# A decoder layer on one core: the expert layer's VectorE work in another order, with sums taken a slot later and v operands made in two steps

## The chip, the cores and the metric

The kernel runs on one core of one Trainium2 chip. The metric is the device time of one execution in microseconds. A core has five engines that each run their own instruction queue in order: TensorE (PE, matrix products into PSUM; its weight loads have a row of their own, PEld), VectorE (DVE), ScalarE (ACT), GpSimd (POOL) and SyncE (SP, which here only issues transfers). Sixteen DMA engines move data between HBM and the on-chip memory. An engine that meets an instruction whose input isn't there yet stands still, and everything behind it in its queue waits too.

## What is computed

One layer over 512 tokens of width 2048: norm, projections, a gated recurrent mixer, a sparse attention mixer, an output projection, and then an expert layer (PEER). Each token picks 128 of 16384 experts (8 heads of 16), each expert being one row of `u` and one row of `v`. The change touches only this layer:

```python
def peer(x, wq, keys1, keys2, u, v):
    ...
    expert = jnp.take_along_axis(cand_i, pos, axis=-1).reshape(t, -1)      # (512, 128)
    gate = jax.nn.softmax(top_s, axis=-1).reshape(t, -1)
    def chunk(args):
        xc, ec, gc = args
        z = jnp.einsum('cd,ced->ce', xc, u[ec])
        act = jax.nn.gelu(z, approximate=False) * gc
        return jnp.einsum('ce,ced->cd', act, v[ec])
    ...
```

## The kernel before

The expert layer is computed in two ways at once. For the first 176 tokens (three row sets of 128, 32 and 16 tokens) the chosen rows are fetched: one indirect transfer brings 128 rows of 2048 numbers, 1.05 MB, into one of three buffers named `rows` (`issue`), and one DVE operation of `use` multiplies and sums it. There are 352 such gathers. `gather(rate)` adds `rate` to a credit at each slot and runs one `use` for every whole credit, so the gathers are spread evenly between the other work.

For the other 336 tokens every expert is computed: `u_tile(i)` is z = gelu(u x) for the 128 experts of tile i, in two pieces of 24 matmuls, and `v_piece(g, pc)` multiplies the gated z of the eight tiles of group g with one piece of v, 24 matmuls again. A matmul here has a 128x128 weight and 336 columns. There are 128 u tiles and 16 v groups of 16 pieces. In this document a slot is the time of one piece. The order is u0 to u33, v0, then two u tiles between two v groups up to v3, u40 to u42, v4, and from there eight u tiles and one v group in turn, v14 behind u122 and v15 at the end.

Full precision comes from splitting each factor into a rounded hi part and the lo part that is left, and three products (`mm3`; lines L167, L168 and L169 are its hi times hi, hi times lo and lo times hi). A weight piece is loaded by SP into `raw`, ACT makes `whi` (L107), DVE subtracts to get `wlo` (L108), and PE uses both. `Pieces.next` gives PE its piece and, ahead of that piece's matmuls in program order, makes both parts of the piece two further on and loads three beyond that. For tiles u0 to u4 POOL makes the lo part in DVE's place.

z isn't ready for v when it leaves PE: it must be multiplied by the gates, and split. `make_a(i)` does all of it at once: DVE multiplies (L962), ACT makes `ah` (L107), DVE makes `al` (L108). `make_some` calls it in the u slots, one tile a slot in the steady part and three a slot in the tiles up to u39. z of the first 40 tiles is spilled to HBM and read back by `load_z`. The gates in expert order are the G matrix; while tiles u5 to u26 run, PE builds it from one-hot vectors that DVE makes for four tokens at a time (`g_batch`; `e1` L1020, `e2` L1021), and it is stored to HBM and read back in a block per group by `load_g`.

A v piece's 128x336 sum is added to `yT` by DVE straight behind its matmuls (L990), but for every fourth piece, which stays in PSUM. When the gathers have ended, after tile u124, `side_load` adds the partial sums of the two small row sets together in five halving steps, and `side_out` norms and stores one row set behind each of u125 to u127. `quarter` transposes, adds and norms the dense tokens at the end.

Of the kernel before, what the change touches and what calls it, by code (L numbers as in the profile page):

```python
# [17 lines left out]
D = 2048  # L18
# [20 lines left out]
class Pieces:  # L39


    def __init__(self, nc, raws, parts, plan, split, load_ahead, split_ahead):
        self.nc, self.raws, self.parts, self.plan, self.split = nc, raws, parts, plan, split
        self.la, self.sa = load_ahead, split_ahead
        self.raw, self.out = {}, {}
        self.loaded = self.done = self.cur = 0
        self.after = {}
        self.extra = None

# [12 lines left out]
    def split_to(self, n):  # L62
        while self.done < min(n, len(self.plan)):
            self.load_to(self.done + 1)
            r, w = self.raw.pop(self.done)
            hi = self.parts.tile([128, 1024], F32R, name="whi")
            lo = self.parts.tile([128, 1024], F32R, name="wlo")
            self.split(hi[:, :w], lo[:, :w], r[:, :w], self.plan[self.done][2])
            self.out[self.done] = (hi, lo)
            self.done += 1  # L70

    def next(self, key, ahead=None):
        assert self.plan[self.cur][0] == key, (self.plan[self.cur][0], key)
        i = self.cur
        self.cur += 1
        self.load_to(i + 1)
        self.split_to(i + 1 + (self.sa if ahead is None else ahead))
        self.load_to(i + 1 + self.la)
        return self.out.pop(i)


def program(tc, a, out):
# [68 lines left out]
    W = Pieces(nc, raws, parts, plan, split, 5, 2)  # L151
# [780 lines left out]
    def u_tile(i, fill, mid=None):  # L932
        p = pw.tile([128, 512], F32, name="pw")
        for hf in range(2):
            whi, wlo = W.next(("u", i, hf))
            for j in range(8):
                k = hf * 8 + j
                cs = slice(j * 128, (j + 1) * 128)
                mm3(p[:, :ND], whi[:, cs], wlo[:, cs], *dense(k), k == 0, k == KT - 1)
                if mid and j % 2:  # L940
                    mid()
            step(fill)
        z = ep["z"].tile([128, ND], F32, name="z")
        nc.scalar.activation(z, p[:, :ND], AF.Gelu)
        if i < NZ:
            nc.scalar.dma_start(zd[i], z)
        else:
            ZR[i] = z
# [5 lines left out]
    def load_z(i):  # L954
        if i < NZ:
            z = ZR[i] = ep["z"].tile([128, ND], F32, name="z")
            nc.sync.dma_start(z, zd[i])

    def make_a(i):
        z = ZR.pop(i)  # L960
        zv = z.rearrange("p (c t) -> p c t", c=NCH)
        nc.vector.tensor_tensor(out=zv, in0=zv, in1=GI[i // 8][:, :, i % 8], op=OP.mult)  # L962
        ah = ep["zp"].tile([128, ND], F32R, name="ah", bufs=9)
        al = ep["zp"].tile([128, ND], F32R, name="al", bufs=9)
        split(ah, al, z)
        AR[i] = (ah, al)


    RES = {}

    def v_piece(g, pc):
# [12 lines left out]
        if res and g == NG - 1:  # L984
            yo = RES[pc] = ep["z"].tile([128, ND], F32, name="z")
# [3 lines left out]
        elif not res:  # L989
            nc.vector.tensor_tensor(out=yo, in0=yo, in1=p[:, :ND], op=OP.add)  # L990
# [13 lines left out]
    def g_batch(tok):  # L1004
# [43 lines left out]
    ep = {"z": pool(zs, "zearly", 2, side="right")}  # L1048

# [95 lines left out]
    RG = 0.3  # L1145
# [4 lines left out]
    def gather_v():  # L1150
        gather(rate)
# [27 lines left out]
    ep["z"] = pool(ev, "z", 8, side="right")  # L1179
# [11 lines left out]
    side = deque((w, st[4], st[5], st[6]) for w, st in enumerate(SETS))  # L1191

    def side_load():
        nc.gpsimd.dma_start(gl, bcast_row(a["gfin"], D))

        for _, y, R, _ in list(side)[1:]:
            n = 64
            while n >= R:
                x = lp.tile([128, D], F32, name="rows", bufs=3)
                nc.gpsimd.dma_start(x[:n], y[n:2 * n])  # L1200
                nc.vector.tensor_tensor(out=y[:n], in0=y[:n], in1=x[:n], op=OP.add)
                n //= 2
# [4 lines left out]

    def side_out():
        w = side.popleft()
        for d in range(4):  # L1210
            normed(*w[:3], d)
        final_out(*w)

    def normed(w, X, P, d):
# [3 lines left out]
        sq = ep["z"].tile([128, ND], F32, name="z")[:, :256].bitcast(BF16)  # L1218
# [34 lines left out]
    def make_some(n, stop):  # L1253
        while n and made[0] < stop and made[0] in ZR:
            make_a(made[0])
            made[0] += 1
            n -= 1
# [3 lines left out]
    rate = (len(seq) - st_["used"]) / (2 * (124 - i) + KT * (NG - 1))  # L1261
    for kind, n in order[i:]:
        if kind == "u":
            if n == U0 - 3:
                load_g(0)
            if n == U0 - 2:
# [11 lines left out]
            if n > 124 and side:  # L1278
                side_out()
        else:  # L1280
            make_some(8, n * 8 + 8)
            assert made[0] >= n * 8 + 8
# [3 lines left out]
            for pc in range(KT):  # L1286
                if pc == 2:
                    load_g(n + 1)
                if pc == 9:
# [6 lines left out]
    assert not side  # L1296

    g = NG - 1
    for pc in range(KT):
        v_piece(g, pc)  # L1300
# [66 lines left out]
```

## Time and profile before

| | us |
|---|---|
| median of 3 runs | 3595.46 |
| lowest and highest | 3591.84, 3596.07 |
| the profiled execution | 3595.78 |
| its span | 3594.0 |

The profile follows one execution. The span runs from its first to its last recorded instruction; the execution's own time is 1.78 us longer. Rows count only busy time of an engine, so what an engine lost shows as the difference between a stretch and its busy time, and the view of the waits puts each idle piece down to the instruction that ended it. The stretches by the trace's clock: one-hot stage about 1500 to 1717, the early groups (v0 to v3) 1770 to 2210, the steady groups 2210 to 3446, the end 3446 to 3577, and then the last transposes, norms and stores.

### The profile page before, as it was taken

To read this page: it belongs to the slowest core of one execution; us is meant where nothing else is said; L and a number is where in the kernel's file an instruction comes from. 1 tells how busy PE (TensorE), PEld (TensorE's weight loads), DVE (VectorE), ACT (ScalarE), POOL (GpSimd) and SP (SyncE) were. 2 spreads that over 40 slices of the span, in tenths; PEclk is the share of its full clock that TensorE was granted. 3 is DMA by queue.
4 is the path that set the end of the run, shared out by engine and by line. 5 is a ranking of instruction groups with operands and counts; after the bars stand their busy time and mean duration, and the time that the engine had idled before them with its cause. 6 is when DMAs were issued, how large, how long until landed. Compare 5 with 4: busy or idle time off the path is not lost.

```text
span 3594.0 us, 50928 instructions
## 1 busy us (share of the span) xinstructions
PE 3451.9 (96%) x19965; PEld 3200.5 (89%) x19965; DVE 2664.0 (74%) x4378; ACT 1296.8 (36%) x1873; POOL 790.7 (22%) x595
## 2 busy tenths in 40 slices
PE   8999999999999999999999999999999999999977
PEld 7988888888888888899999889999999999999977
DVE  6778755444443369999778888888888888878875
ACT  5555554333332332344333322333333333323333
POOL 4200000000010055500122232332332232223210
PEclk9999999999999999999999999999999999999989
DMA  5323322222224352577899998999999999999973
GB/s 191 117 88 100 96 93 90 84 79 77 82 95 141 116 150 89 169 259 264 340 348 352 359 377 332 379 356 355 377 368 348 348 387 357 344 351 382 358 265 112
DMA packets 215137, 860.35 MB, mean 239 GB/s; under 512 B 22992, under 2 KB 65104, under 8 KB 166640
## 3 DMA queue, kind: packets, MB, share of 16 engines
q1 hardware_dynamic: 147824, 439.21, 34.2%
q0 software_dynamic: 59440, 388.97, 27.9%
q10 hardware_dynamic: 7632, 28.91, 2.1%
q8 instruction: 156, 2.56, 0.3%
q14 instruction: 85, 0.70, 0.1%
HBM read 811.54 MB, written 36.64 MB: 236 GB/s over the span
## 4 chain that ended last, share of the span: by engine, by line
PE 42%; DVE 11%; issue 5%; ACT 3%; DMA 3%; POOL 1%; SPq 0%; ACTq 0%; POOLq 0%; DVEq 0%
PE pw L169 10%; PE pw L167 10%; PE pw L168 10%; DVE wlo L108 4%; ACT whi L107 2%; DVE rows L1130 2%; PE pg L1029 2%; DVE x1A L1136 2%; PE pr L167 2%; PE pr L168 2%; PE pr L169 2%; PE acc L169 2%; PE acc L168 2%; PE acc L167 2%; DVE z L962 1%
## 5 line engine op out<-in xcount | busy, mean ns | idle before, releaser
L108 DVE TENSOR_TENSOR wlo<-raw,whi 128x1024 fp32r<-128x1024 f32 (+1 forms) x712 | 864.0, 1217 | 470.3 <-ACT whi L107 468.0
L107 ACT CAST whi<-raw 128x1024 fp32r<-128x1024 f32 (+1 forms) x752 | 780.1, 1040 | 984.9 <-PE pw L168 364.1
L169 PE MATMUL pw<-h2m,wlo 128*128 128x336 f32 x2048 | 658.2, 321 | 46.6 <-DVE wlo L108 40.8
L167 PE MATMUL pw<-h2m,whi 128*128 128x336 f32 x2048 | 662.9, 324 | 19.0 <-ACT whi L107 18.4
L167 PE MATMUL pw<-ah,whi 128*128 128x336 f32 x1536 | 492.8, 321 | 24.3 <-ACT whi L107 12.8
L169 PE MATMUL pw<-ah,wlo 128*128 128x336 f32 x1536 | 493.1, 321 | 11.6 <-DVE wlo L108 11.6
L168 PE MATMUL pw<-al,whi 128*128 128x336 f32 x1536 | 491.2, 320 | 0.5
L167 PE MATMUL acc<-hTh,whi 128*128 128x512 f32 (+1 forms) x1152 | 444.9, 386 | 0.8 <-ACT nts L370 0.8
L168 PE MATMUL acc<-hTl,whi 128*128 128x512 f32 (+1 forms) x1152 | 443.2, 385 | 2.3 <-DVE hTl L270 2.3
L169 PE MATMUL acc<-hTh,wlo 128*128 128x512 f32 (+1 forms) x1152 | 444.0, 385 | 0.0
L169 PEld LDWEIGHTS pw<-h2m,wlo 128*128 128x128 f32 x2048 | 389.1, 190 | 59.1 <-DVE wlo L108 52.5
L167 PEld LDWEIGHTS pw<-h2m,whi 128*128 128x128 f32 x2048 | 390.4, 191 | 26.3 <-ACT whi L107 26.0
L168 PE MATMUL pw<-h2m,whi 128*128 128x336 f32 x1024 | 326.8, 319 | 0.0
L1116 POOL DMA_INDIRECT rows<-in_u,ex x128 | 191.3, 1495 | 613.0 <-DVE rows L1130 550.9
L168 PE MATMUL pw<-h2r,whi 128*128 128x336 f32 x1024 | 325.8, 318 | 0.0
L167 PEld LDWEIGHTS pw<-ah,whi 128*128 128x128 f32 x1536 | 294.1, 191 | 28.6 <-ACT whi L107 14.5
L1136 DVE SCALAR_TENSOR_TENSOR x1A<-rows,zgA,x1A 128x2048 f32<-128x2048 f32 x128 | 300.2, 2345 | 10.1 <-DMA rows<-in_v,ex 10.1
L169 PEld LDWEIGHTS pw<-ah,wlo 128*128 128x128 f32 x1536 | 293.6, 191 | 15.3 <-DVE wlo L108 14.9
L1130 DVE SCALAR_TENSOR_TENSOR rows<-rows,h2g 128x2048 f32<-128x2048 f32 x128 | 292.3, 2284 | 10.2 <-DMA rows<-in_u,ex 10.1
L168 PEld LDWEIGHTS pw<-al,whi 128*128 128x128 f32 x1536 | 294.2, 192 | 2.6 <-DVE al L108 2.6
L1116 POOL DMA_INDIRECT rows<-in_v,ex x128 | 184.7, 1443 | 436.0 <-DVE x1A L1136 345.6
L168 PEld LDWEIGHTS acc<-hTl,whi 128*128 128x128 f32 x1152 | 216.4, 188 | 45.4 <-DVE hTl L270 3.0
(363 smaller groups left out, 6027.6 us busy)
## 6 DMA issues: line engine op xcount, KB each, us to landing
raw<-in_ut SPq DMA_DIRECT2D x256, 512.0 KB, 6.3
raw<-in_vt SPq DMA_DIRECT2D x256, 512.0 KB, 8.0
raw<-in_wt SPq DMA_DIRECT2D x144, 512.0 KB, 3.5
gd<-stg ACTq DMA_DIRECT2D x12, 1792.0 KB, 7.0
gi<-gd SPq DMA_DIRECT2D x16, 1344.0 KB, 17.1
raw<-in_wo SPq DMA_DIRECT2D x32, 512.0 KB, 3.2
raw<-in_wq SPq DMA_DIRECT2D x32, 512.0 KB, 3.2
raw<-in_wukv SPq DMA_DIRECT2D x16, 512.0 KB, 3.2
```

What stands on the lines that cost most here:

```text
L107: nc.scalar.copy(hi, src)
L108: (lo_eng or nc.vector).tensor_tensor(out=lo, in0=src, in1=hi.bitcast(F32), op=OP.subtract)
L167: nc.tensor.matmul(p, ahi, bhi, start=start, stop=False)
L168: nc.tensor.matmul(p, ahi, blo, start=False, stop=False)
L169: nc.tensor.matmul(p, alo, bhi, start=False, stop=stop)
L962: nc.vector.tensor_tensor(out=zv, in0=zv, in1=GI[i // 8][:, :, i % 8], op=OP.mult)
L1029: nc.tensor.matmul(p[:, j * 128:(j + 1) * 128], e1[:, j], e2[:, j], start=True, stop=True)
L1116: nc.gpsimd.indirect_dma_start(out=r, out_offset=None, in_=a[kind], in_offset=bass.IndirectOffsetOnAxis(ap=SETS[w][0][:, s:s + 1], axis=0))
L1130: nc.vector.scalar_tensor_tensor(r, r, 1.0, hg, op0=OP.mult, op1=OP.mult, accum_out=zg[:, s:s + 1])
L1136: nc.vector.scalar_tensor_tensor(y, r, zg[:, s:s + 1], y, op0=OP.mult, op1=OP.add)
```

## The change

- `Pieces` makes hi and lo parts apart. From u0 on (`defer`) `next` asks ACT for the hi part of the piece two ahead, and `finish`, at the end of a slot, makes its lo part and loads five pieces further in place of three where the two extra buffers exist.
- `make_a` is cut in three: `make_mul` in one slot, `make_hi` and `make_lo` in the next.
- `v_piece` hands its addition back, and the next slot does it first.
- `slot` sets DVE's order in a slot: the last piece's sums, multiplies, gathers, `al`, and then the lo part.
- Gather rates: 0.55 a slot in place of 0.3 in the one-hot stage, none in tiles u32 to u39, 0.756 in other u slots and 0.826 in v slots; what is left after u121 is done there at once (before: after u124).
- `e1` of four tokens is made by one operation.
- The halving sums, norms and stores of the row sets are a generator, `folds`, one step in each slot from u122 on; the two sets' steps alternate.
- `load_g(0)` and the first `load_z` stand a tile earlier, later ones two pieces earlier; z has a name of its own for tiles that are spilled.

```diff
@@ class Pieces @@
...
+    def finish(self):
+        n = self.cur + self.sa
+        self.lo_to(n)
+        self.load_to(n + 3 + (NRAW2 if self.extra else 0))
@@ def next @@
-        self.split_to(i + 1 + (self.sa if ahead is None else ahead))
-        self.load_to(i + 1 + self.la)
+        if self.defer:
+            self.lo_to(i + 1)
+            self.hi_to(i + 1 + self.sa)
+        else:
+            self.split_to(i + 1 + (self.sa if ahead is None else ahead))
+            self.load_to(i + 1 + self.la)
         return self.out.pop(i)
@@ def v_piece @@
         elif not res:
-            nc.vector.tensor_tensor(out=yo, in0=yo, in1=p[:, :ND], op=OP.add)
+            return [lambda: nc.vector.tensor_tensor(out=yo, in0=yo, in1=p[:, :ND], op=OP.add)]
+        return []
@@ def one_hot @@
+            if js[0] == 0:
+                B = [128, 4, 128]
+                nc.vector.tensor_tensor(out=e1, in0=iota[:, None, :].to_broadcast(B),
+                                        in1=iT[:, 0, j0:j0 + 4, None].to_broadcast(B), op=OP.is_equal)
             for j in js:
                 t = j0 + j
-                nc.vector.tensor_scalar(e1[:, j], iota, iT[:, 0, t:t + 1], None, op0=OP.is_equal)
...
+    W.finish()
+    W.defer = True
...
-    RG = 0.3
+    RG = 0.55
...
+    def folds():
         nc.gpsimd.dma_start(gl, bcast_row(a["gfin"], D))
+        n, got = 64, []
+        while True:
+            for y, x, m in got:
+                nc.vector.tensor_tensor(out=y[:m], in0=y[:m], in1=x[:m], op=OP.add)
...
+            n //= 2
+            yield
...
+    def slot(rate, muls=()):
+        while adds:
+            adds.popleft()()
+        old = list(fin)
+        fin.clear()
+        for i in muls:
+            make_mul(i)
+        for i in old:
+            make_hi(i)
+        gather(rate)
+        for i in old:
+            make_lo(i)
...
-    rate = (len(seq) - st_["used"]) / (2 * (124 - i) + KT * (NG - 1))
+    between = range(U0 - 2, NZ)
+    nu = 2 * len([n for n in range(i, 122) if n not in between])
+    RU = (len(seq) - st_["used"] - 0.07 * KT * (NG - 1)) / (nu + KT * (NG - 1))
+    RV = RU + 0.07
...
             def fill():
-                gather_v()
-                make_some(3 if n < NZ else 1, min((group + 1) * 8, n))
+                stop = min((group + 1) * 8, n)
+                k = 3 if n in between else 1
+                muls = [j for j in range(made[0], min(made[0] + k, stop)) if j in ZR]
+                made[0] += len(muls)
+                slot(0 if n in between else RU, muls)
+                if n > 121:
+                    next(side, None)
             u_tile(n, fill)
-            if n == 124:
+            if n == 121:
                 while st_["used"] < len(seq):
                     use()
-                side_load()
...
-                v_piece(n, pc)
-                step(gather_v)
+                add = v_piece(n, pc)
+                slot(RV)
+                adds.extend(add)
+                W.finish()
```

Three places show the moved order on DVE. The first is a u group in the steady part, behind v13; before, each slot begins with the lo part and then has a gather, a multiply and `al` of the same z:

```order
L108 TENSOR_TENSOR wlo_29406<-raw_29308,whi_29405 128x1024
L1136 SCALAR_TENSOR_TENSOR yB_12283<-rows_29336,zgS0_12285,yB_12283 128x2048
L962 TENSOR_TENSOR z_28721<-z_28721,gi_28925 128x336
L108 TENSOR_TENSOR al_29440<-z_28721,ah_29439 128x336
L108 TENSOR_TENSOR wlo_29444<-raw_29343,whi_29443 128x1024
L1136 SCALAR_TENSOR_TENSOR yB_12283<-rows_29371,zgS0_12285,yB_12283 128x2048
L962 TENSOR_TENSOR z_28787<-z_28787,gi_28925 128x336
L108 TENSOR_TENSOR al_29478<-z_28787,ah_29477 128x336
```

The same place after the change:

```order
L79 TENSOR_TENSOR wlo_29135<-raw_28994,whi_29134 128x1024
L992 TENSOR_TENSOR z_28479<-z_28479,gi_28685 128x336
L1180 SCALAR_TENSOR_TENSOR yB_12283<-rows_29093,zgS0_12285,yB_12283 128x2048
L79 TENSOR_TENSOR wlo_29167<-raw_29028,whi_29166 128x1024
L992 TENSOR_TENSOR z_28548<-z_28548,gi_28685 128x336
L1180 SCALAR_TENSOR_TENSOR yB_12283<-rows_29128,zgS0_12285,yB_12283 128x2048
L1003 TENSOR_TENSOR al_29229<-z_28479,ah_29228 128x336
L79 TENSOR_TENSOR wlo_29201<-raw_29062,whi_29200 128x1024
```

The multiply now opens the slot, `al` (of z_28479) comes a slot behind its multiply, and the lo part closes the slot.

The second place is DVE at the first multiplies, those for v0; before, they stand in u32:

```order
L108 TENSOR_TENSOR wlo_15509<-raw_15390,whi_15508 128x1024
L1130 SCALAR_TENSOR_TENSOR rows_15452,zgA_12284<-rows_15452,h2g_8662 128x2048
L962 TENSOR_TENSOR z_15491<-z_15491,gi_15419 128x336
L108 TENSOR_TENSOR al_15543<-z_15491,ah_15542 128x336
L962 TENSOR_TENSOR z_15493<-z_15493,gi_15419 128x336
L108 TENSOR_TENSOR al_15548<-z_15493,ah_15547 128x336
L962 TENSOR_TENSOR z_15495<-z_15495,gi_15419 128x336
L108 TENSOR_TENSOR al_15553<-z_15495,ah_15552 128x336
L108 TENSOR_TENSOR wlo_15557<-raw_15426,whi_15556 128x1024
```

After the change they begin in u31, whose two slots have one multiply each:

```order
L992 TENSOR_TENSOR z_15206<-z_15206,gi_15137 128x336
L1174 SCALAR_TENSOR_TENSOR rows_15128,zgA_12284<-rows_15128,h2g_8662 128x2048
L79 TENSOR_TENSOR wlo_15224<-raw_15062,whi_15223 128x1024
L992 TENSOR_TENSOR z_15208<-z_15208,gi_15137 128x336
L1174 SCALAR_TENSOR_TENSOR rows_15197,zgA_12284<-rows_15197,h2g_8662 128x2048
L1003 TENSOR_TENSOR al_15286<-z_15206,ah_15285 128x336
L79 TENSOR_TENSOR wlo_15258<-raw_15099,whi_15257 128x1024
L992 TENSOR_TENSOR z_15210<-z_15210,gi_15137 128x336
L992 TENSOR_TENSOR z_15212<-z_15212,gi_15137 128x336
```

Lo parts and one gather a slot still lie between them in u31; from u32 on the gathers are gone and three multiplies stand together. The z loads are issued right ahead of the tile of the first multiply in both.

The third place is the end of the gathers on DVE; before, no gather is left over and five halving sums stand together between two lo parts, near u125:

```order
L108 TENSOR_TENSOR al<-z,ah 128x336
L1201 TENSOR_TENSOR yB<-yB,rows 64x2048
L1201 TENSOR_TENSOR yB<-yB,rows 32x2048
L1201 TENSOR_TENSOR h2gB<-h2gB,rows 64x2048
L1201 TENSOR_TENSOR h2gB<-h2gB,rows 32x2048
L1201 TENSOR_TENSOR h2gB<-h2gB,rows 16x2048
L108 TENSOR_TENSOR wlo<-raw,whi 128x1024
```

After the change, behind u121 (x13 is thirteen of them in a row):

```order
L79 TENSOR_TENSOR wlo<-raw,whi 128x1024
L1180 SCALAR_TENSOR_TENSOR h2gB<-rows,zgS_12286,h2gB 128x2048 x13
L79 TENSOR_TENSOR wlo<-raw,whi 128x1024
L1239 TENSOR_TENSOR yB<-yB,rows 64x2048
L1239 TENSOR_TENSOR h2gB<-h2gB,rows 64x2048
L79 TENSOR_TENSOR wlo<-raw,whi 128x1024 x2
```

The halving sums come two to a slot, and thirteen gathers stand between two lo parts.

## Rows read from the trace of the kernel before

**Rows 1.** Busy time, share of the span and instructions of each engine.
```profile
PE 3451.9 (96%) x19965; PEld 3200.5 (89%) x19965; DVE 2664.0 (74%) x4378; ACT 1296.8 (36%) x1873; POOL 790.7 (22%) x595
```
**Rows 2.** Windows: stretch, us, busy PE, PEld, DVE, ACT, POOL, PEclk, DMA, GB/s.
```profile
1450.00:1500.00 50.00, 43.27 (x246) 42.36 (x245) 44.94 (x161) 17.17 (x22) 30.77 (x24) 0.86 0.33 112
...
1500.00:1717.00 217.00, 216.18 (x1573) 215.64 (x1573) 210.73 (x680) 94.72 (x139) 28.12 (x29) 1.00 0.72 262
...
1770.00:2210.00 440.00, 405.71 (x2495) 395.89 (x2494) 362.22 (x362) 135.19 (x172) 123.11 (x85) 0.95 0.93 358
...
2210.00:3446.00 1236.00, 1200.84 (x7680) 1183.47 (x7679) 1066.51 (x964) 388.57 (x487) 375.76 (x270) 0.99 0.94 362
...
3446.00:3577.00 131.00, 105.13 (x663) 103.23 (x663) 81.33 (x108) 47.47 (x85) 6.98 (x11) 0.91 0.45 143
...
2395.00:2454.00 59.00, 59.00 (x386) 59.00 (x385) 53.18 (x47) 17.21 (x17) 21.00 (x13) 1.00 1.01 399
2454.00:2518.00 64.00, 61.09 (x390) 59.61 (x389) 53.26 (x56) 21.72 (x32) 14.61 (x14) 1.00 0.89 335
```
**Rows 3.** PE's waits (us, times, longest): first 1770-2210, then 2210-3446, then 3446-3577.
```profile
PE pw L167 <- ACT whi L107: 21.2, 7, 7.1
...
PE pw L169 <- DVE wlo L108: 26.8, 35, 5.8
...
PE pw L169 <- DVE wlo L108: 19.4, 3, 18.4
```
**Rows 4.** Timeline 2213-2218: start, us, instruction, [idle before <-releaser].
```profile
2214.87 0.50 DVE L962 TENSOR_TENSOR z<-z,gi 128x336 f32<-128x336 f32 x1
...
2215.40 0.47 ACT L107 CAST ah<-z 128x336 fp32r<-128x336 f32 x1 [4.53 <-DVE z L962]
...
2215.78 1.04 ACT L107 CAST whi<-raw 128x1024 fp32r<-128x1024 f32 x1
...
2215.91 0.51 DVE L108 TENSOR_TENSOR al<-z,ah 128x336 fp32r<-128x336 f32 x1 [0.54 <-ACT ah L107]
...
2216.86 1.23 DVE L108 TENSOR_TENSOR wlo<-raw,whi 128x1024 fp32r<-128x1024 f32 x1 [0.44 <-ACT whi L107]
```
**Rows 5.** DVE's waits in 1770-3446 (us, times, longest).
```profile
DVE wlo L108 <- ACT whi L107: 94.3, 140, 3.4
...
DVE al L108 <- ACT ah L107: 67.7, 120, 0.9
...
DVE yT L990 <- PE pw L169: 38.3, 40, 3.5
...
DVE z L962 <- DMA z<-zd: 7.7, 1, 7.7
```
**Rows 6.** DVE's groups in 2210-3446: busy, mean ns | idle before, releaser.
```profile
L108 DVE TENSOR_TENSOR wlo<-raw,whi 128x1024 fp32r<-128x1024 f32 x320 | 389.8, 1221 | 68.6 <-ACT whi L107 67.6 <-PE pw L168 0.4
...
L1136 DVE SCALAR_TENSOR_TENSOR x1A<-rows,zgA,x1A 128x2048 f32<-128x2048 f32 x94 | 220.5, 2346 | 7.1 <-DMA rows<-in_v,ex 7.1
...
L990 DVE TENSOR_TENSOR yT<-yT,pw 128x336 f32<-128x336 f32 x120 | 59.8, 498 | 26.5 <-PE pw L169 26.1
```
**Rows 7.** DVE's timeline in the one-hot stage.
```profile
1604.39 0.28 DVE L1020 TENSOR_SCALAR e<-iota,gT 128x128 f32<-128x128 f32 x1
1604.59 0.34 DVE L1021 TENSOR_SCALAR e<-iota,gT 128x128 f32<-128x128 f32 x1
```
**Rows 8.** A 128x512 operation of DVE, near the end (L1244), as a group.
```profile
L1244 DVE TENSOR_TENSOR rows<-rows,pw 128x512 f32<-128x512 f32 x8 | 5.4, 684 | 3.8 <-PE pw L1243 3.8
```
**Rows 9.** DMA in 1770-3446: totals, then gathers (count, median us from issue to landing).
```profile
DMA packets 141296, 604.63 MB, mean 361 GB/s; under 512 B 13328, under 2 KB 44110, under 8 KB 98473
...
rows<-in_v,exS POOLq DMA_INDIRECT x48, 9.6
```
**Rows 10.** DVE's timeline 3000-3016: two gathers in a row.
```profile
3006.93 2.34 DVE L1136 SCALAR_TENSOR_TENSOR x1A<-rows,zgA,x1A 128x2048 f32<-128x2048 f32 x1
...
3010.32 2.35 DVE L1136 SCALAR_TENSOR_TENSOR x1A<-rows,zgA,x1A 128x2048 f32<-128x2048 f32 x1
```

More of the change, by code (lines that the diff above doesn't have):

```diff
@@ L955, in load_z, with make_mul, make_hi, make_lo @@
         if i < NZ:
-            z = ZR[i] = ep["z"].tile([128, ND], F32, name="z")
+            z = ZR[i] = ep["z"].tile([128, ND], F32, name="z", bufs=8)
             nc.sync.dma_start(z, zd[i])
-    def make_a(i):
-        z = ZR.pop(i)
+    mul, fin = deque(), deque()
+    def make_mul(i):
+        z = ZR[i]
         zv = z.rearrange("p (c t) -> p c t", c=NCH)
         nc.vector.tensor_tensor(out=zv, in0=zv, in1=GI[i // 8][:, :, i % 8], op=OP.mult)
-        ah = ep["zp"].tile([128, ND], F32R, name="ah", bufs=9)
-        al = ep["zp"].tile([128, ND], F32R, name="al", bufs=9)
-        split(ah, al, z)
+        fin.append(i)
+    def make_hi(i):
+        ah = ep["zp"].tile([128, ND], F32R, name="ah", bufs=8)
+        al = ep["zp"].tile([128, ND], F32R, name="al", bufs=8)
         AR[i] = (ah, al)
+        nc.scalar.copy(ah, ZR[i])
+    def make_lo(i):
+        ah, al = AR[i]
+        nc.vector.tensor_tensor(out=al, in0=ZR.pop(i), in1=ah.bitcast(F32), op=OP.subtract)
     RES = {}
+    adds = deque()
     def v_piece(g, pc):
@@ L984, in v_piece @@
         if res and g == NG - 1:
-            yo = RES[pc] = ep["z"].tile([128, ND], F32, name="z")
+            yo = RES[pc] = ep["z"].tile([128, ND], F32, name="z", bufs=8)
             nc.scalar.copy(yo, p[:, :ND])
@@ L1190, in program @@
     XD = []
-    side = deque((w, st[4], st[5], st[6]) for w, st in enumerate(SETS))
-    def side_load():
+    def folds():
         nc.gpsimd.dma_start(gl, bcast_row(a["gfin"], D))
[L1196 to L1202, printed above, removed]
+        n, got = 64, []
+        while True:
+            for y, x, m in got:
+                nc.vector.tensor_tensor(out=y[:m], in0=y[:m], in1=x[:m], op=OP.add)
+            got = []
+            for st in SETS[1:]:
+                if n >= st[5]:
+                    x = lp.tile([128, D], F32, name="rows", bufs=3)
+                    nc.gpsimd.dma_start(x[:n], st[4][n:2 * n])
+                    got.append((st[4], x, n))
+            if not got:
+                break
+            n //= 2
+            yield
         for row, P in CHK:
@@ L1206, in side_load @@
             XD.append(x)
[L1208 to L1212, printed above, removed]
+        for w, st in enumerate(SETS):
+            for d in range(4):
+                if d % 2 == 0:
+                    yield
+                normed(w, st[4], st[5], d)
+            yield
+            final_out(w, *st[4:7])
+    side = folds()
     def normed(w, X, P, d):
@@ L1217, in normed @@
         r = rf[:P, w:w + 1]
-        sq = ep["z"].tile([128, ND], F32, name="z")[:, :256].bitcast(BF16)
+        sq = ep["z"].tile([128, ND], F32, name="z", bufs=8)[:, :256].bitcast(BF16)
         nc.scalar.activation(sq[:P], X[:P, ds_], AF.Square, accum_out=fs[:P, w, d:d + 1])
@@ L1288, in program @@
                     load_g(n + 1)
-                if pc == 9:
+                if pc == 7:
                     for j in range(8):
                         load_z(n * 8 + 8 + j)
-                v_piece(n, pc)
-                step(gather_v)
+                add = v_piece(n, pc)
+                slot(RV)
+                adds.extend(add)
+                W.finish()
             for j in range(8):
                 AR.pop(n * 8 + j)
-    assert not side
     g = NG - 1
     for pc in range(KT):
-        v_piece(g, pc)
+        adds.extend(v_piece(g, pc))
+        slot(0)
+        next(side, None)
+        W.finish()
         if pc % 4 == 0 and pc:
```

65 lines of the change are left out of this document (37 added, 28 removed).

## The prediction

> **What bounds the kernel now.** I read the engine totals first, then the busy time by stage, then what TensorE (PE) waits for, then the in-order queues of VectorE (DVE) and ScalarE (ACT) around such a wait. PE is busy 96% of the span [rows 1], so about 140 us is all that any reordering can win. By stage [rows 2]: in the v group at 2395-2454 PE issues 386 matmuls in 59.00 us without a gap, 0.153 us each, and I take that as the floor. 1770-2210 holds 2495 matmuls, floor 382, so 58 us are lost; 2210-3446 holds 7680, floor 1175, 61 lost; 3446-3577 holds 663 (some 40 of them short transposes), floor about 100, 31 lost. The one-hot stage (1500-1717) loses nothing: its 1573 matmuls, many of them short, leave PE no gap, and DVE is busy 210.73 of 217 us.
>
> The waits [rows 3] say who is late: first ACT's hi part of a weight piece (21.2 us in seven waits), then DVE's lo part (26.8 us in 35), at the end one wait that makes up 18.4 of 19.4 us. How it comes shows in a u group in [rows 4]: DVE multiplies z at 2214.87; ACT can't make ah before 2215.40 and had stood still 4.53 us, with the next hi part queued behind it; DVE stands 0.54 us for ah, and another 0.44 us for that hi part. DVE loses 94.3 us to the hi parts, 67.7 us to ah and 38.3 us to sums that wait for PE [rows 5]: 200 us in 1676, while its work nearly fills the time. So DVE's order is the bound of the dense part, not its work. DMA is the neighbour to watch: share 1.01 and 399 GB/s in the v group [rows 2].
>
> **The change, part by part.** A slot is one piece of PE work, 24 matmuls, 3.7 us.
>
> *Two steps, last piece's sums, lo last.* A slot's DVE work now needs only what ACT and PE finished a slot earlier; the lo part of the piece two ahead ends the slot instead of opening it. Its hi part is then long made, so the three waits of [rows 5] go. What is late next is DVE's work itself, by the durations in [rows 4, 6]: a u group takes 16 x 1.22 (lo) + 8 x 1.01 (z, al) + 12.1 x 2.35 (gathers, at the new rate 0.756 a slot) = 56 of 59 us; its first nine slots, which hold all eight z and al, 35.1 of 33.2, so DVE falls 1.9 us back, under the slot of slack that a piece two ahead has. A v group takes 16 x 1.22 + 12 x 0.50 + 13.2 x 2.35 (rate 0.826) = 56.5 of 59. It fits, with little to spare. Behind a late row now stands the lo part as well: it was done some 2.3 us into a slot (hi 1.05, lo 1.22), needed at 7.3, and is now done at about 4.1 (0.50 + 2.35 + 1.22), so slack falls from 5.0 to 3.2 us.
>
> *Early groups (58 lost).* Between v0 and v3 the kernel needs eight z, al in four u slots. Before, a full slot held 3 x (0.50 + 0.54 + 0.51) + 0.44 + 1.23 + 0.79 x 2.35 = 8.2 us of DVE for 3.7 us of PE. Now gathers stay out and the waits go: 3 x 1.01 + 1.22 = 4.3 in the fullest, 13 in 14.7 over the four. The granted clock of 0.95 in this stretch [rows 2], a mix of both levels, should come back to 1.00 with the gaps. What stays is the first z: DVE waited 7.7 us for it [rows 5], its load is issued a tile earlier, but its multiply now also stands a tile earlier, so the distance is the same. I leave 17 us (8 for that z, the rest as in the steady part): **-41**. Bounds: -27 and -52.
>
> *Steady groups (61 lost).* The u groups lose some 47 of these (the one at 2454-2518 took 64 us where the v group took 59 [rows 2]). I leave 8 there. The longest single wait, 5.8 us [rows 3], comes where a gather queues on GpSimd (POOL) behind loads for the second row set; that order stays: 8 with what follows. Other: 4. The v groups get 0.65 gathers more each, 0.68 MB on 23.5 MB that already ran at share 1.01: nothing if 399 GB/s isn't the end, 1.7 us a group if it is, half of it taken, 8 for ten groups. Left 28: **-33**, bounds -10 and -48.
>
> *One-hot stage.* DVE's busy time is 10.72 us a tile (210.73 x 80 matmuls / 1573) for PE's 11.04. Four e1 at a pitch of 0.20 [rows 7] become one 128x512 operation of 0.68 [rows 8]: -0.46 a tile for four batches. The gather rate of 0.55 for 0.3 adds 0.5 x 2.35 = 1.18. So 11.43, 0.39 over PE, 8.6 us in 22 tiles, of which a slot's slack hides about 5: **+4**, bounds 0 and +14. It moves 11 of the 352 gathers here, where DMA has room (0.72 [rows 2]).
>
> *Queues.* Once the two extra buffers exist, five pieces are in flight instead of three: weight loads queue deeper against the gathers (rival 2), and the z and gate loads stand behind them on SyncE's queue, issued 8 or more slots (30 us) ahead of use in all groups but the first, against a landing of some 10 us as the gathers show [rows 9], so covered. For u0 to u4 POOL makes the lo parts, and there they now follow the expert multiplies in its queue; PE loses 6.7 of 50 us in 1450-1500 [rows 2], by the same POOL, and I take 0, bounds -4 and +4.
>
> *The end.* The rate for the last gathers counts 15 v groups, but only 14 come before tile u121: 22 + 174 x 0.756 + 224 x 0.826 = 339 of 352, and the order shows the remaining 13 back to back on DVE. This is a new stall. Three row buffers: bounds are DVE alone, 13 x 2.35 = 30.5 us, and landing, 13 x (9.6 + 2.35) / 3 = 52 us [rows 6, 9]. Nearest is the pace of [rows 10], 3.39 us a gather with no wait for rows: 2 x 2.35 + 11 x 3.4 = 42. PE has two pieces in stock, 7.3 us, and needs a lo part (1.2) after: 36 of stall, and about 3 more as the next lo part stands behind two fold adds. Against that the serial fold of before (18.4 us of PE's wait [rows 3]) and most of the rest of 31 go; 6 stay for the last u group. 39 + 6 - 31 = **+14**, bounds 0 and +25.
>
> **Sum** on the profiled execution: 3594.0 - 41 - 33 + 4 + 14 = 3538 of span, and 1.8 around it as now (3595.78 - 3594.0): 3539.8. The median of the runs shown, 3595.46, is 0.3 under the profiled one: **3540 us**. The last quarter's transposes, norms and stores after 3577 aren't touched.
>
> **Rivals.** (1) *DMA is the bound.* 1770-3446 moves 604.63 MB at 361 GB/s [rows 9]. If that mean can't rise, only bytes moved out count: 11 rows of 1.05 MB, 11.5 MB, 32 us, against +18 for one-hots and burst: about 3580. For it: share 1.01 in v groups, 0.94 overall. Against: u groups run at 0.89, and a v group held 399 GB/s for 59 us; the new demand is 377 (32 pieces of 0.52 MB, 25.3 rows of 1.05 and a gate block of 1.38 make 44.7 MB in two groups of 59.2 us). The Trainium skill's page DMA: Bandwidth & Descriptors (Specifications) gives a limit of about 358 GB/s of memory to a core; by that the dense part couldn't get faster at all. The v group in [rows 2] disagrees. Chance 12%.
>
> (2) *Slower: three row buffers set the pace.* Every lo part now stands behind a gather, and five weight pieces in flight may delay rows. A buffer's turn is landing + 0.3 + 2.35; with three, 310 gathers between 1770 and the burst take as long as PE does now, less the 18 above, at 5.35 us each, a landing of 13.4 us. At 14 us: 310 x 5.55 = 1720 for 1676, +44 + 18: about 3656. Against: the median landing is 9.6 us [rows 9], and DVE's waits for rows are small (7.1 us for 94 gathers [rows 6]). Chance 5%.
>
> (3) *The waits only change their name*: DVE, over 95% filled, falls behind in u groups as before; steady and early groups win a third: -25 + 18, about 3588. Chance 5%.
>
> (4) *Better than forecast*: the burst near its lower bound and the dense part at its floor: about 3500. Chance 5%.
>
> **How the numbers follow.** Forecast 3510 to 3564: 73%. With the nearer half of rival 1 the range 3510 to 3580 holds 8 in 10. About 0.2% (7 us) is what a measurement of this kernel can tell from no change. Faster by more: forecast, rivals 1 and 4, part of 3: 0.91. Within: 0.04. Slower: 0.05.
>
> **What would show it.** Right: DVE's waits for hi parts, ah and PE under 60 us together; u groups of 59 to 60 us, v groups under 61; granted clock 1.00 through 1770-3400; one stall of 25 to 45 us before the last v groups, released by a lo part behind 13 gathers. Wrong: DMA share 1.0 with v groups over 62 us (rival 1), DVE waiting over 100 us for rows (rival 2), u groups still 63 us (rival 3), or no long stall at the end.

## The result, and the profile after

The changed kernel takes 3529.93 us (median of 4 runs, 3527.58 to 3531.33) where the kernel before takes 3595.77 (4 runs, 3591.84 to 3596.66): a ratio of 0.9818, interval 0.9801 to 0.9835. The profiled execution has a span of 3525.8 us, 68.2 less than before. The forecast was 3540, range 3510 to 3580.

The page's engine totals, as in [rows 1]: the span shrinks, DVE's work stays nearly the same, PE has 97% of the span.

```profile
PE 3414.4 (97%) x19965; PEld 3188.5 (90%) x19965; DVE 2631.9 (75%) x4126; ACT 1299.7 (37%) x1873; POOL 843.2 (24%) x595
```

The windows answer to [rows 2]: stretch, length, busy time of PE, PEld, DVE, ACT and POOL with instruction counts, PE's granted clock, DMA share, GB/s. The first is the one-hot stage, the second v0 to v4, the third the steady part up to v14, one v group of it, then v14, and then two pieces of v14.

```profile
1500.00:1717.00 217.00, 216.00 (x1574) 215.62 (x1573) 216.39 (x472) 92.35 (x140) 42.35 (x35) 1.00 0.85 308
...
1802.00:2167.00 365.00, 363.52 (x2355) 362.49 (x2354) 315.58 (x312) 123.86 (x155) 109.30 (x73) 1.00 0.97 374
2167.00:3300.00 1133.00, 1126.71 (x7297) 1125.87 (x7297) 1009.83 (x926) 377.69 (x470) 401.83 (x258) 1.00 0.98 377
...
2345.00:2404.00 59.00, 59.00 (x385) 59.00 (x384) 51.35 (x48) 17.15 (x18) 19.93 (x13) 1.00 1.00 394
...
3300.00:3406.00 106.00, 63.10 (x389) 62.55 (x389) 59.87 (x46) 17.45 (x18) 18.62 (x14) 0.81 0.65 216
...
3334.00:3339.00 5.00, 0.00 (x0) 0.00 (x0) 3.07 (x2) 0.00 (x0) 0.42 (x1) 0.50 1.01 346
3340.00:3350.00 10.00, 5.99 (x30) 5.71 (x29) 6.91 (x5) 1.05 (x1) 1.00 (x2) 0.84 0.78 166
```

From v0 to the start of v14 PE issues a matmul every 0.155 us (365 / 2355, and 1133 / 7297), where a v group at the floor has one every 0.154 (59.1 / 384): some 12 us are lost in 1498. v14 takes 106 us where the group before it takes 59. PE stands still there; at the end of the stall the granted clock is 0.50, the lower of the two levels, and then 0.84, a mix of both, before it comes back to 1.00.

PE's waits, as in [rows 3], in three stretches: 1700 to 1810, 2167 to 3300, 3300 to 3510 (us in total, times, longest).

```profile
PE pw L193 <- DVE wlo L79: 10.9, 1, 10.9
...
PE pw L193 <- DVE wlo L79: 6.2, 2, 5.4
...
PE pw L193 <- DVE wlo L79: 42.9, 2, 38.9
```

Four waits are left that matter (10.9, 5.4, and 38.9 and 4.0 in v14), and these rows name a lo part each time. What stood ahead of that lo part on DVE is seen in its timeline (start, us, instruction, idle before and releaser), first at the first z, then at the end of the gathers, with SyncE's row (SPq) that issued the z loads between:

```profile
1768.68 1.22 DVE L79 TENSOR_TENSOR wlo<-raw,whi 128x1024 fp32r<-128x1024 f32 x1
1781.96 0.51 DVE L992 TENSOR_TENSOR z<-z,gi 128x336 f32<-128x336 f32 x1 [12.06 <-DMA z<-zd]
...
1770.59 11.64 SPq L984 DMA_DIRECT2D z<-zd  x8
...
3297.76 2.35 DVE L1180 SCALAR_TENSOR_TENSOR h2gB<-rows,zgS,h2gB 128x2048 f32<-128x2048 f32 x1 [2.68 <-DMA rows<-in_v,exS]
...
3335.93 2.35 DVE L1180 SCALAR_TENSOR_TENSOR h2gB<-rows,zgS,h2gB 128x2048 f32<-128x2048 f32 x1 [2.76 <-DMA rows<-in_v,exS]
3338.20 1.22 DVE L79 TENSOR_TENSOR wlo<-raw,whi 128x1024 fp32r<-128x1024 f32 x1
```

DVE's waits in 1770 to 3300 answer to [rows 5]; its third row, a multiply that waits for ACT's gelu, has no counterpart there.

```profile
DVE wlo L79 <- ACT whi L70: 44.0, 49, 3.2
DVE yT L1028 <- PE pw L193: 35.1, 32, 1.5
DVE z L992 <- ACT z L975: 19.2, 19, 1.2
...
DVE al L1003 <- ACT ah L999: 12.5, 26, 1.4
DVE z L992 <- DMA z<-zd: 12.1, 1, 12.1
```

And this is DVE in a u group, as in [rows 4]: multiply, gather, `al` of the z before, lo part. None of the eight rows has a bracket, so DVE had no idle time before any of them.

```profile
2175.89 1.22 DVE L79 TENSOR_TENSOR wlo<-raw,whi 128x1024 fp32r<-128x1024 f32 x1
2177.02 0.50 DVE L992 TENSOR_TENSOR z<-z,gi 128x336 f32<-128x336 f32 x1
2177.44 2.35 DVE L1180 SCALAR_TENSOR_TENSOR x1A<-rows,zgA,x1A 128x2048 f32<-128x2048 f32 x1
2179.70 0.50 DVE L1003 TENSOR_TENSOR al<-z,ah 128x336 fp32r<-128x336 f32 x1
2180.12 1.22 DVE L79 TENSOR_TENSOR wlo<-raw,whi 128x1024 fp32r<-128x1024 f32 x1
2181.26 0.50 DVE L992 TENSOR_TENSOR z<-z,gi 128x336 f32<-128x336 f32 x1
2181.68 0.50 DVE L1003 TENSOR_TENSOR al<-z,ah 128x336 fp32r<-128x336 f32 x1
2182.10 1.22 DVE L79 TENSOR_TENSOR wlo<-raw,whi 128x1024 fp32r<-128x1024 f32 x1
```

Where the 68.2 us went, and those of the experiments, shows when each profiled execution is cut at the first matmul of v0, the end of v4, the start and the end of v14 and the end of v15. A v group at the floor takes 59.1 us. The stretch behind v15 is 17 us in all of them.

| us | up to v0 | v0 to v4 | to v14 | v14 | u123 to v15 |
|---|---|---|---|---|---|
| before | 1804.2 | 405.6 | 1177.4 | 58.9 | 130.9 |
| after | 1802.1 | 364.9 | 1133.1 | 105.6 | 103.1 |
| end_v14 | 1803.8 | 364.5 | 1127.8 | 59.2 | 109.0 |
| rate_14 | 1802.4 | 370.5 | 1134.4 | 59.4 | 103.1 |
| z_row_early | 1803.7 | 367.8 | 1126.9 | 106.8 | 103.1 |
| best1 | 1804.3 | 364.1 | 1132.6 | 59.2 | 109.7 |
| lo_first | 1806.0 | 370.3 | 1131.6 | 102.3 | 100.1 |
| one_step | 1805.9 | 382.3 | 1140.9 | 106.9 | 106.0 |
| add_now | 1801.1 | 386.0 | 1161.7 | 104.2 | 103.1 |
| order_undone | 1810.2 | 393.0 | 1182.8 | 102.7 | 109.5 |
| depth_3 | 1798.1 | 362.6 | 1132.0 | 102.6 | 103.1 |
| gather_between | 1803.3 | 380.5 | 1129.8 | 101.8 | 103.1 |
| best2r | 1799.1 | 366.5 | 1136.5 | 59.2 | 110.5 |
| best3 | 1796.6 | 362.5 | 1129.2 | 59.2 | 109.3 |

So the change won 2.1 us ahead of v0, 40.7 in v0 to v4, 44.3 in the steady part and 27.8 at the end, and lost 46.7 in v14. No run puts the old serial halving sums back into the changed kernel, so what won the 27.8 isn't shown by itself.

### The profile page after: what moved, and what is told of

The parts are those of the page before. It is cut to its first block, busy times and chain, and to the rows that moved or that the text cites. A ratio compares the mean times of both kernels' runs of the same rounds, so it can differ in the third digit from the quotient of the medians.

```text
span 3525.8 us, 50708 instructions
## 1 busy us (share of the span) xinstructions
PE 3414.4 (97%) x19965; PEld 3188.5 (90%) x19965; DVE 2631.9 (75%) x4126; ACT 1299.7 (37%) x1873; POOL 843.2 (24%) x595
## 3 DMA queue, kind: packets, MB, share of 16 engines
q0 software_dynamic: 59440, 388.97, 28.6%
## 4 chain that ended last, share of the span: by engine, by line
PE 43%; DVE 14%; DMA 4%; issue 2%; POOL 1%; ACT 0%; ACTq 0%; POOLq 0%; SPq 0%; DVEq 0%
PE pw L193 12%; PE pw L191 12%; PE pw L192 12%; DVE e L1063 2%; PE pr L193 2%; PE pr L191 2%; PE pr L192 2%; DVE rows L1174 2%; DVE wlo L79 2%; DMA rows<-in_v,exS 2%; DVE e L1059 1%; DVE idx L937 1%; DVE i L854 1%; DVE v L850 1%; DMA raw<-in_ut 1%
## 5 line engine op out<-in xcount | busy, mean ns | idle before, releaser
L79 DVE TENSOR_TENSOR wlo<-raw,whi 128x1024 fp32r<-128x1024 f32 (+1 forms) x712 | 865.4, 1218 | 405.6 <-ACT whi L70 404.7
L193 PE MATMUL pw<-h2m,wlo 128*128 128x336 f32 x2048 | 649.4, 317 | 16.5 <-DVE wlo L79 10.9
L1160 POOL DMA_INDIRECT rows<-in_v,ex x128 | 211.5, 1653 | 374.7 <-DVE x1A L1180 268.5
```

The source lines that it names most:

```text
L79: self.plan[self.los][2].tensor_tensor(out=lo[:, :w], in0=r[:, :w], in1=hi[:, :w].bitcast(F32), op=OP.subtract)
L193: nc.tensor.matmul(p, alo, bhi, start=False, stop=stop)
L1160: nc.gpsimd.indirect_dma_start(out=r, out_offset=None, in_=a[kind], in_offset=bass.IndirectOffsetOnAxis(ap=SETS[w][0][:, s:s + 1], axis=0))
```

## The experiments

The theory to test: VectorE's order in a slot was the bound of the dense part, and it is lifted because no step waits any more for what another engine makes in the same slot. Rival A: weight loads five pieces ahead feed PE better. Rival B: the gain comes from moving gathers, out of tiles u32 to u39 and into the one-hot stage. All edits are made to the changed kernel.

**One part undone: the lo part opens the slot again.**

```diff
-            self.lo_to(i + 1)
-            self.hi_to(i + 1 + self.sa)
+            self.lo_to(i + 1 + self.sa)
```

> The changed kernel, but the lo part opens a slot again, straight behind its hi part. In before, VectorE lost 94.3 us to hi parts in the dense part. If lo last is what won the steady groups, most of their 51 us come back: 3560-3580. My view: the wait limits itself, since a VectorE that is half a slot behind finds the hi part done; with the other two waits gone, 0 to +10: 3530-3540.

Measured 3527.97 us, ratio 0.9813 (0.9797 to 0.9829): no difference from the changed kernel. DVE's waits in 2167 to 3300 for hi parts are 84.8 us here, and u and v groups still take 59 us (windows of one u and one v group):

```profile
DVE wlo L79 <- ACT whi L70: 84.8, 83, 2.5
...
2413.00:2472.00 59.00, 59.00 (x386) 59.00 (x385) 52.49 (x55) 22.18 (x32) 15.42 (x13) 1.00 0.96 355
2472.00:2531.00 59.00, 59.00 (x384) 59.00 (x384) 53.21 (x41) 17.20 (x17) 21.89 (x14) 1.00 1.00 397
```

These waits for hi parts are waits of an engine that is ahead, and cost nothing while it stays ahead. The 94.3 us of [rows 5] were not 94.3 us to be won.

**One part undone: multiply, `ah` and `al` of a z in one go.**

```diff
-        old = list(fin)
-        fin.clear()
-        for i in muls:
-            make_mul(i)
-        for i in old:
-            make_hi(i)
         gather(rate)
-        for i in old:
-            make_lo(i)
+        for i in muls:
+            make_mul(i)
+            make_hi(i)
+            make_lo(i)
+        fin.clear()
```

> The changed kernel, but z's multiply, ah and al stand together in one slot again behind the gather. VectorE must wait 0.54 us for ah each time, however late it is: 4.3 us in a u group of 56, all in its first nine slots (39.4 us of work in 33.2), 6 us behind where a slot of slack hides some 4: 10 to 30 us, 3540-3560. If two steps were idle: 3528-3533.

Measured 3561.47 us, ratio 0.9904 (0.9885 to 0.9922): 31.5 us more than the changed kernel, just over the upper end. By the table 17.4 of them are in v0 to v4, where a slot makes three z, and 7.8 in the steady part. DVE's waits have the old row again, at the same half microsecond each, in 2167 to 3300 and in 1806 to 2188, its v0 to v4:

```profile
DVE al L1003 <- ACT ah L999: 42.7, 78, 0.6
...
DVE al L1003 <- ACT ah L999: 17.3, 32, 0.5
```

Where three z a slot fill DVE, 17.3 us of such waits stand beside 17.4 us lost; in the steady part, where DVE has room, 42.7 us of them stand beside 7.8.

**One part undone: the sum of a v piece in its own slot.**

```diff
                 add = v_piece(n, pc)
+                adds.extend(add)
                 slot(RV)
-                adds.extend(add)
```

> The changed kernel, but a v piece's sum is added in its own slot, ahead of the gather and the lo part. VectorE then starts a slot's work only when PE ends the piece: 0.50 + 2.35 + 1.22 = 4.07 us later the lo part is there, which PE wants 4.0 us later. So the slack in v groups is gone: 0.1 to 0.2 us lost in some ten slots of a group and each late row in full, 2 to 4 us a v group: 3555-3590. Rival: the loads ahead and the spread gathers did it, and VectorE's order in v groups doesn't matter: 3528-3535.

Measured 3574.58 us, ratio 0.9945 (0.9928 to 0.9961), 44.7 more than the changed kernel. DVE's wait for PE is 110.5 us in 2167 to 3300, and now it is the v group that is long; the u group beside it takes its 59.5 us:

```profile
DVE yT L1028 <- PE pw L193: 110.5, 48, 5.1
...
2428.00:2488.00 60.00, 60.00 (x389) 59.56 (x388) 56.02 (x57) 22.28 (x32) 19.82 (x15) 1.00 0.99 385
2488.00:2550.00 62.00, 60.89 (x384) 58.71 (x383) 51.30 (x40) 17.15 (x17) 20.27 (x13) 1.00 0.90 347
```

**All three undone together.** The three edits above in one kernel.

> All three orders undone together (lo part first, one step for z, sum in its own slot); loads five ahead, gather rates, gathers kept out of u32 to u39, one-hots and the end stay as changed. If VectorE's order is what won the steady groups (51 us), this gives them back, and more because the gather rate is higher: 3570-3600. If deeper loads or the spread of the gathers won it: 3530-3545.

Measured 3618.88 us, ratio 1.0068 (1.0051 to 1.0085): 89 us more than the changed kernel and slower than the kernel before. The steady part takes 1182.8 us, before 1177.4. That settles rivals A and B for this part: loads five ahead and the new gather rates stayed, and the whole gain is gone, so by themselves they win nothing there. In v0 to v4 28.1 of the 40.7 us are gone. The windows show where: a u group of 63 us again, and a v group of 59.

```profile
2449.00:2512.00 63.00, 60.68 (x385) 59.01 (x385) 52.64 (x55) 21.77 (x32) 17.81 (x14) 1.00 0.86 324
2512.00:2571.00 59.00, 59.00 (x385) 59.00 (x384) 53.16 (x42) 17.18 (x17) 23.45 (x14) 1.00 1.02 407
```

Set beside add_now this tells more. In the steady part a sum in its own slot costs a v group some 3 us when the lo part stands behind it (28.6 us over nine groups), and nothing when the lo part stands ahead of it, as before and here. So in these v groups two edits of the change, lo part last and sum a slot later, only pay for each other. In the u groups it is the other way round: with either the lo part last (one_step: 7.8 us lost in the steady part) or two steps (lo_first: none) most of the loss is gone, and only with neither is it all back. Two steps with lo parts first and sums in their own slot, the smallest version that these runs point to, wasn't tried.

**Loads three ahead.**

```diff
-        self.load_to(n + 3 + (NRAW2 if self.extra else 0))
+        self.load_to(n + 3)
```

> The changed kernel with weight loads three pieces ahead as before, not five. If five in flight is what feeds TensorE at 377 GB/s, the steady groups lose time again: 3550 and more. My view: loads are released by the lo part that frees a buffer, the landing takes some 10 us, and three pieces are 11 us of work, so the hi parts wait a little for their pieces: 0 to +10, 3528-3540.

Measured 3519.95 us, ratio 0.9792 (0.9775 to 0.9808). That is against rival A altogether, and better than I expected: the ratio is 0.0026 under the changed kernel's, some 9 us, though the intervals overlap. The table has 4.0 of it ahead of v0, 2.3 in v0 to v4 and 3.0 in v14, all stretches where gathers, z or gate blocks move beside the weights; that the weights held these up isn't shown.

**Gathers in u32 to u39 too.**

```diff
-    nu = 2 * len([n for n in range(i, 122) if n not in between])
+    nu = 2 * (122 - i)
...
-                slot(0 if n in between else RU, muls)
+                slot(RU, muls)
```

> The changed kernel with gathers also in tiles u32 to u39, at a rate lowered for it (0.73 and 0.80 a slot), so that as many are left over at the end as in the changed kernel. Some 12 gathers, 27 us of VectorE, come into eight tiles where z's three multiplies a slot already take 4.3 of 3.7 us. If keeping them out is what won the early groups: +15 to +30, 3545-3560, with the loss between v0 and v4. If the waits for hi parts and ah were the cause there, and two steps cure that: 3528-3535.

Measured 3537.87 us, ratio 0.9842 (0.9825 to 0.9858): 7.9 more than the changed kernel, between the two expectations. In the place itself it cost 15.6 us (v0 to v4, 380.5 for 364.9), and the lower rate elsewhere gave back 3.3 in the steady part and 3.8 in v14. So rival B holds for some 15 of the 41 us of v0 to v4, and the order for some 28 (order_undone); together they are a little more than the whole.

**The end: the same rates, what is left done behind v14.**

```diff
-    nu = 2 * len([n for n in range(i, 122) if n not in between])
+    nu = 2 * len([n for n in range(i, 123) if n not in between])
...
-                if n > 121:
+                if n > 122:
                     next(side, None)
             u_tile(n, fill)
-            if n == 121:
-                while st_["used"] < len(seq):
-                    use()
...
                 AR.pop(n * 8 + j)
+            if n == NG - 2:
+                while st_["used"] < len(seq):
+                    use()
```

> Same gather rates as the changed kernel, but what is left is done behind v14 and not behind u121; the halving sums start in u123. If the 13 gathers in a row are the whole loss at v14 (46.4 us over the floor of 0.154 us a matmul), the group goes back to about 59 to 61 us and the time from 3530 to 3484-3492. Rival: the halving sums, now beside v15's own norms, stall PE as they did before (some 18 us): 3500-3508.

Measured 3483.90 us, ratio 0.9684 (0.9668 to 0.9700). u122's slots are counted now, which lowers the rates by 0.003, and v14's own 16 slots take the 13 gathers at 0.82 a slot, so that none has to be done in a row. v14 takes 59 us, and the halving sums beside u123 cost 5.9 us (109.0 for 103.1):

```profile
3296.00:3355.00 59.00, 59.00 (x385) 59.00 (x384) 51.63 (x41) 17.19 (x17) 17.66 (x13) 1.00 1.00 377
3355.00:3464.00 109.00, 104.25 (x661) 102.66 (x661) 74.80 (x106) 47.42 (x85) 8.56 (x10) 0.97 0.49 154
```

**The end: a rate that leaves none over.**

```diff
-    RU = (len(seq) - st_["used"] - 0.07 * KT * (NG - 1)) / (nu + KT * (NG - 1))
+    RU = (len(seq) - st_["used"] - 0.07 * KT * (NG - 2)) / (nu + KT * (NG - 2))
```

> The gather rate counts the 14 v groups that do come before u121: about 0.79 a u slot and 0.86 a v slot, 0.55 gathers more in each group of 16 slots, none left over. VectorE's own work is then 57.8 of 59.2 us in a v group. If VectorE's work is the only bound, nothing else moves: 3480-3490. If DMA is near its end (share 1.00 at 394 GB/s in v groups), each v group grows by up to 1.4 us and rows come late: 3495-3515.

Measured 3496.41 us, ratio 0.9719 (0.9703 to 0.9736): the time of the second case, but not its place. No v group of the steady part grew (1134.4 us for 1133.1, and 399 GB/s in a group); v0 to v4 did, by 5.6 us, where PE waits for `al` (2.5 us), lo parts (1.8) and hi parts (1.3). The profiled execution took 3488.59 and was the fastest; what the others lost beyond it no trace shows.

**The two other stalls: the first z, and the loads for the third row set.** First both loads earlier (z_row_early), then with the end mended (best1), then with the multiplies held where they were and the row set's loads spread (best2r).

```diff
-            if n == U0 - 4:
+            if n == U0 - 6:
                 load_g(0)
-            if n == U0 - 3:
+            if n == U0 - 5:
                 for j in range(8):
                     load_z(j)
@@ use @@
+        issue(k + 3)
         for f in before.pop(k, ()):
             f()
-        issue(k + 3)
@@ best2r alone: use @@
+        k0 = seq.index(("u", 1, SETR[0] - 1)) + 1
+        for q, f in enumerate(set_input(2)):
+            before.setdefault(k0 + q, []).append(f)
@@ best2r alone: fill @@
-                muls = [j for j in range(made[0], min(made[0] + k, stop)) if j in ZR]
+                muls = [j for j in range(made[0], min(made[0] + k, stop)) if j in ZR and n >= U0 - 3]
```

> The changed kernel with the first gate and z loads issued two tiles earlier and the next gather issued ahead of the loads for a new row set. The two stalls left outside the end are 11.1 us (the first z, landed 12 us after VectorE asked for it) and 5.6 us (a gather's transfer behind eight small loads on GpSimd's queue), and 12.8 and 8.1 us with the lower clock behind them. If these are causes, both go: 3507-3514. If the waits are contention for DMA, they come back elsewhere: 3520-3530.

> end_v14 and z_row_early together. The places are apart, so the gains should add: 3484-3492 less 16 to 20, about 3466-3474. If gathers that come earlier only meet other transfers, less than the sum: 3475-3485.

> end_v14, with the first gate and z loads two tiles earlier but the first multiplies where they were (u31), so that this time the distance grows by two tiles, and with the loads for the third row set spread over as many gathers, each behind the next gather's issue. z's wait was 11.4 us with the clock's part 14.3, the row's 4: if both are queueing, 3484 - 14 - 4, about 3464-3472. If z's loads are late because all transfers are at their limit there, 3478-3486.

Measured 3526.45 (ratio 0.9798), 3487.65 (0.9694) and 3489.52 us (0.9705), each with an interval of about 0.0016 to either side: the first in its second case, the other two above both of theirs and no faster than end_v14. In z_row_early the reason is my edit: a multiply is made as soon as its z is loaded, so it moved forward with the load, as it had in the change itself, and DVE's row is the old one 13 us earlier:

```profile
1768.97 0.51 DVE L992 TENSOR_TENSOR z<-z,gi 128x336 f32<-128x336 f32 x1 [15.93 <-DMA z<-zd]
```

With the multiply held (best2r) the wait for z is gone, but ACT then waits for weight pieces, and v0 begins 4.7 us earlier than in end_v14. At the row set, in v12, the results go both ways. The gather's issue ahead of the loads made v12, from its first matmul to the next group's, shorter in z_row_early (61.9 us for the changed kernel's 67.2), but longer in best1 (68.1 for end_v14's 63.3), so that this order is the cause isn't shown. With the loads spread over eight gathers (best2r) v12 takes 72.0 us: PE waits 9.8 us for a hi part, whose weights were under way together with those loads and the next group's gate block. The transfers of 3050 to 3100 in best2r (count, KB each, median us to landing), and ACT's row:

```profile
raw<-in_vt SPq DMA_DIRECT2D x9, 512.0 KB, 18.6
gi<-gd SPq DMA_DIRECT2D x1, 1344.0 KB, 32.2
...
3094.92 1.04 ACT L70 CAST whi<-raw 128x1024 fp32r<-128x1024 f32 x1 [18.85 <-DMA raw<-in_vt]
```

Weights that took 18.6 us to land were late as transfers, on a queue whose order I hadn't changed. Which of the other transfers held them, these rows don't tell.

**Put together:** end_v14, loads three ahead, z loaded one to a slot. As in best2r, the first gate block is also loaded two tiles earlier and the first multiply held in u31.

```diff
-        self.load_to(n + 3 + (NRAW2 if self.extra else 0))
+        self.load_to(n + 3)
...
+                if U0 - 6 <= n < U0 - 2:
+                    load_z(len(zl))
+                    zl.append(n)
```

> end_v14 with loads three pieces ahead, and the first eight z loaded one to a slot from u28 on in place of eight at once, the first multiply staying in u31. depth_3 gained 10 us on the changed kernel, some 6 of it outside the thirteen gathers; the first z's stretch lost 14.3 us in end_v14 and 10.2 in best2r, where SyncE needed 11.4 us to issue the eight loads. If issuing them all at once into full queues is the cause: 3484 - 6 - 11, about 3464-3470. If that stretch is held by the amount of transfers, however they are spaced: 3474-3480.

Measured 3476.01 us, ratio 0.9668 (0.9655 to 0.9682), the fastest of all: 119 us under the kernel before and 54 under the changed one. It is the second case: v0 begins 7.2 us earlier than in end_v14, but PE still waits 4.0 us there for a hi part. SyncE's queue is slow here too: the first z behind the gate block needs 11.32 us to be issued, the next ones 0.3 to 0.5.

```profile
1742.92 0.38 SPq L979 DMA_DIRECT2D gi<-gd  x1
1743.35 11.32 SPq L984 DMA_DIRECT2D z<-zd  x1
1754.77 0.59 SPq L58 DMA_DIRECT2D raw<-in_ut  x1
1755.41 0.45 SPq L984 DMA_DIRECT2D z<-zd  x1
```

The gate block stands right ahead of that z, but the six weight loads ahead of the block took 13.82 us to issue, so the rows don't tell which of them made it wait.

## Why the prediction was right

- *The bound.* Right, and shown by order_undone: with DVE's old order the steady part is back at its old length, whatever else stays changed. But the reading of the three waits of [rows 5] as 200 us of loss was too simple, and they didn't go: 94.3, 67.7 and 38.3 us became 44.0, 12.5 and 35.1. lo_first keeps the wait for hi parts, at 84.8 us, and loses nothing. Put back alone, the wait for `ah` costs 31.5 us (one_step): DVE can't get out of it by being late, at half a microsecond each. The wait for PE costs 44.7 us (add_now), but only with the lo part behind it.
- *v0 to v4: forecast -41, measured -40.7.* Right in size; the two causes, waits and gathers, share it as 28 and 15 us in order_undone and gather_between. The first z did wait at least as long as before, 12.1 us for 7.7, because multiply and load moved together; that cost falls ahead of v0, while the forecast's stretch began at 1770 and so held it, with 8 of the 17 us it left; PE waits 10.9 us there. To the end of v4 the kernel is 42.8 us earlier.
- *Steady part: forecast -33, bounds -10 and -48, measured -44.3.* The mis-sized terms are what I left in it. The 8 us for u groups were nothing: the lag of 1.9 us in the first nine slots stays under the slack. The 8 us for v groups at the limit of DMA were nothing as well: they run at 394 GB/s and share 1.00 without a gap. The longest wait, left at 8, is what stayed, at the loads for the third row set (the prediction says the second): 5.4 us and the clock behind it, in a v12 of 67.2 us.
- *One-hot stage: forecast +4.* The sum had DVE over PE by 0.39 us a tile; it is full, at 216.39 of 217 us, but not over. The gathers' rows, before and after:

```profile
L1130 DVE SCALAR_TENSOR_TENSOR rows<-rows,h2g 128x2048 f32<-128x2048 f32 x10 | 22.8, 2278 | 0.0
...
L1174 DVE SCALAR_TENSOR_TENSOR rows<-rows,h2g 128x2048 f32<-128x2048 f32 x19 | 43.7, 2299 | 0.0
```

Nine gathers more are 20.9 us, and DVE's busy time rose by 5.7 (210.73 to 216.39), so the one-hots gave back some 15 us in these 20 tiles, nearly 0.8 a tile where the sum had 0.46. The four-token operation takes 0.70 us, as forecast. PE waits 1.8 us in all for one-hots there, and v0 begins 2.1 us earlier than before, not 4 later. No run undid the operation or the rate of 0.55 by itself.
- *The end: forecast +14, measured +18.9 (46.7 - 27.8).* The 13 gathers in a row, read from the order alone, were there, and the stall's size came close: 42.9 us of waits for 39 forecast. That it came so close was luck. The 3.39 us between the two gathers of [rows 10] weren't a pace of gathers, since a lo part lies between them, which those rows don't show:

```profile
3009.19 1.22 DVE L108 TENSOR_TENSOR wlo<-raw,whi 128x1024 fp32r<-128x1024 f32 x1
```

In the thirteen no lo part lies between, and DVE waits for rows instead, 15.7 us in all: they take 46.7 us (3291.6 to 3338.3), 3.6 each, between the prediction's bounds of 30.5 (DVE alone) and 52 (landing). The rest of v14's loss is PE at the lower clock behind the stall. The 6 us for the last u group did not come: u123 to u127 take 36.9 us for 240 matmuls, the floor.
- *What would show it.* The u groups and the stall came as said, the v groups too but for v12 (67.2 us), and the clock from v0 to v14, where the stall took it down to 0.81 for the group. DVE's waits for hi parts, `ah` and PE are 44.0 + 12.5 + 35.1 = 92 us, not under 60: the wrong measure, since a DVE ahead of its work must wait for something.
- *The rivals.* DMA as the bound (1) falls: 377 GB/s for 1133 us where it would have held 361. The Trainium skill's page DMA: Bandwidth & Descriptors (Specifications) has a limit of about 358 GB/s to a core, which this kernel's traffic exceeds at those 377 GB/s. The same page of the Trainium skill (Bandwidth, Measured) says that each core gets roughly that when both cores of a memory domain stream; this kernel runs on one core, so the prediction's use of it as a bound was a misreading. Row buffers (2): DVE waits 59 us for rows in 1770 to 3300 (35 times, at most 10.9 at once), of which 5.4 reach PE; they set the pace only in the thirteen. Waits that only change their name (3) falls: 92 us of the three waits are left, but the u groups take 59.1 us and not 63.

The errors of the terms (steady part 11 better, what lies ahead of v0 6 better, end 5 worse) make the span 12 us shorter than forecast; the median stands 2.3 us above the profiled execution (3527.58), so 10 are left between 3540 and 3530.

## What to carry to other kernels

An engine that waits is not an engine that costs: ask whether it could be late without anyone noticing. Waits for something that another engine makes out of one's own last result aren't shortened by being late, so they come on top of the engine's own work and cost where that work nearly fills the time: 17.4 us lost for 17.3 of them in v0 to v4, 7.8 for 42.7 in the steady part (one_step). Put other work between, or a slot. And when work is spread by a rate, count the slots that come before its deadline and look in the order for what is left over: here a count of 15 groups for 14 took 46.7 us, two thirds of what the whole change had won.

## What the hardware showed that I had not expected

- A DMA share of 1.00 is no end: at it, v groups ran at 394 GB/s (after) and 407 GB/s (order_undone) without PE losing time.
- Issuing a transfer can itself take long. In best3 the issue behind a gate block of 1344 KB took SyncE 11.32 us, when the block's own issue took 0.38 us and later z loads 0.3 to 0.5 each. In the changed kernel the eight z loads took 11.64 us to issue. Which limit of the queue that is, no run here shows.
- Moving loads earlier gained nothing where the transfers themselves were late: best1 and best2r ran at 3488 and 3490 us, end_v14 without such edits at 3484. Fewer weight loads in flight lost nothing: three pieces ahead ran at 3520 us, five at 3530, with intervals that overlap.
